# SwiGLU on one core: the first two tiles loaded, multiplied and stored row by row

## The chip, the cores and the metric

One core of one Trainium2 chip. The metric is the time of one execution on the device in microseconds (us), the median of several runs. The profile is of one execution; its span runs from the first to the last instruction and is 1 to 2 us shorter than the time. A packet is the piece of a transfer that one DMA engine moves in one go, here what lies together in one partition: 64 KiB in a whole load, 32 KiB in a whole store. Where the text says "packet records", the start and duration of every packet were read from the trace file; no view of the profile prints them.

## The reference

```python
"x": np.random.randn(8192, 8192).astype(np.float32)

def reference(x):
    a, b = np.split(x, 2, axis=-1)
    silu_b = b / (1 + np.exp(-b))
    return a * silu_b
```

Every row of 8192 floats (32 KiB) gives a row of 4096 floats (16 KiB): 268.4 MB are read and 134.2 MB written. ScalarE makes the SILU of the right half, VectorE multiplies it by the left.

## The kernel before

The input is seen as 4096 pairs of rows, the pairs cut into 32 tiles of 128. One tile holds two rows (64 KiB) in each of the 128 partitions, 8.39 MB in all. There are three tile buffers. Loads and the last three stores go out on SyncE's queue (SP), the other thirty stores on ScalarE's (ACT). The product is written over the tile itself, so a buffer is free for the next load only when its store has landed. The last tile is already loaded and stored by rows; the first tiles are not.

```python
R = 2
BUFS = 3
...
def load(i, rows=None):
    if i not in tiles:
        tiles[i] = pool.tile([P, R * M], x.dtype, name="xt")
    lo, hi = (0, R) if rows is None else rows
    nc.sync.dma_start(
        out=tiles[i][:, lo * M : hi * M], in_=xv[i * P : (i + 1) * P, lo * M : hi * M]
    )

def swiglu(i, k, c0=0, cw=half):
    xt = tiles[i]
    b = xt[:, k * M + half + c0 : k * M + half + c0 + cw]
    nc.scalar.activation(out=b, in_=b, func=_SILU)
    nc.vector.tensor_mul(
        out=xt[:, k * half + c0 : k * half + c0 + cw],
        in0=xt[:, k * M + c0 : k * M + c0 + cw],
        in1=b,
    )

def store(i, c0=0, cw=R * half):
    (nc.scalar if i < last - 1 else nc.sync).dma_start(
        out=ov[i * P : (i + 1) * P, c0 : c0 + cw], in_=tiles[i][:, c0 : c0 + cw]
    )

for i in range(BUFS):
    load(i)
for i in range(last):
    for k in range(R):
        swiglu(i, k)
    if i == last - 1:
        swiglu(last, 0)
    store(i)
    nxt = i + BUFS
    if nxt < last:
        load(nxt)
    elif nxt == last:
        load(last, (0, 1))
        load(last, (1, 2))
... # the last tile: store of row 0, row 1 in two halves, store of row 1
```

Of the kernel before, what the change touches and what calls it, by code (L numbers as in the profile page):

```python
# [1 line left out]

# [4 lines left out]

_SILU = mybir.ActivationFunctionType.Silu


@with_exitstack
def kernel(
    ctx: ExitStack,
    tc: tile.TileContext,
    x: bass.AP,
    out: bass.AP,
):




    nc = tc.nc
    N, M = x.shape
    half = M // 2
    P = nc.NUM_PARTITIONS
    R = 2
    BUFS = 3

    xv = x.tensor.reshape([N // R, R * M]).ap()  # L30
    ov = out.tensor.reshape([N // R, R * half]).ap()
    ntiles = N // (P * R)
    last = ntiles - 1

    pool = ctx.enter_context(tc.tile_pool(name="sbuf", bufs=BUFS))
    ctx.enter_context(tc.manual_schedule())
    tiles = {}
# [22 lines that stand above are left out]
        )  # L60

    for i in range(BUFS):
        load(i)
    for i in range(last):
        for k in range(R):
            swiglu(i, k)
        if i == last - 1:
            swiglu(last, 0)
        store(i)
        nxt = i + BUFS  # L70
        if nxt < last:
            load(nxt)
# [4 lines that stand above are left out]
    store(last, 0, half)  # L77
    for c0 in range(0, half, half // 2):
        swiglu(last, 1, c0, half // 2)
    store(last, half, half)  # L80


# [1 line left out]
_INS = ['x']  # L84
_OUTS = [((8192, 4096), 'float32')]


# [23 lines left out]
```

## Time and profile before

| | before |
|---|---|
| time, median (lowest to highest) | 936.18 us (936.04 to 936.34) |
| span of the profiled run | 934.8 us |
| both DMA queues, share of 16 engines | 99.8% |
| VectorE, ScalarE busy | 30%, 25% |
| HBM traffic over the span | 431 GB/s |

The engines that compute have little to do; the 16 DMA engines are busy all the time. In this list of DMA issues of the kernel before, the last number is the median time from issue to landing in us:

```profile
out_dram<-xt ACTq DMA_DIRECT2D x30, 4096.0 KB, 39.7
...
xt<-in_x_dram SPq DMA_DIRECT2D x31, 34.5
```

A whole load (8 MiB, its size isn't printed) takes 34.5 us and a store of 4 MiB takes 39.7, though alone, at 434 GB/s, they would take 19.3 and 9.7. They wait for each other in the queues.

### The profile page before, as it was taken

The page shows a single profiled execution, that of the slowest core. Times are in us where ns is not written, and L with a number is a line of the kernel's source. Part 1 is how long each engine was busy: PE and PEld are TensorE (multiplying, and loading weights), DVE is VectorE, ACT ScalarE, POOL GpSimd, SP SyncE. Part 2 cuts the span into 40 slices and gives each one's busy share as a digit, 9 for nine tenths or more (in the row PEclk, how much of TensorE's full clock was granted, in tenths as well). Part 3 has the DMA queues.
Part 4 walks back from the last instruction along what each step waited for, and adds up shares of the span by engine and source line. Part 5 has one row for each costly group of instructions (what it writes and reads, how often), then busy time and mean ns, then how long its engine had stood idle before and what let it go on. Part 6 is the DMA issues. An engine that isn't in the chain of part 4 may idle for free.

```text
span 934.8 us, 367 instructions
## 1 busy us (share of the span) xinstructions
DVE 283.3 (30%) x65; ACT 229.4 (25%) x66; POOL 0.2 (0%) x4
## 2 busy tenths in 40 slices
DVE  0333312333123331133321333213332133331242
ACT  0223320233302333113331133311333203332041
POOL 0000000000000000000000000000000000000000
DMA  9999999999999999999999999999999999999998
GB/s 404 400 445 430 430 439 433 428 435 443 428 430 439 429 442 432 435 426 453 419 430 452 411 452 423 428 447 425 433 433 453 414 443 429 426 447 428 425 437 376
DMA packets 9506, 402.67 MB, mean 431 GB/s; under 512 B 1056, under 2 KB 1056, under 8 KB 1056
## 3 DMA queue, kind: packets, MB, share of 16 engines
q1 hardware_dynamic: 5184, 276.83, 68.6%
q10 hardware_dynamic: 4320, 125.83, 31.2%
q14 instruction: 2, 0.02, 0.0%
HBM read 268.44 MB, written 134.22 MB: 431 GB/s over the span
## 4 chain that ended last, share of the span: by engine, by line
DMA 84%; DVE 10%; ACT 4%; DVEq 0%; issue 0%; SPq 0%; ACTq 0%
DMA out_dram<-xt 42%; DMA xt<-in_x_dram 42%; DVE xt L51 10%; ACT xt L50 4%; DVEq L106 0%; SPq L43 0%; ACTq L50 0%; DVEq L51 0%
## 5 line engine op out<-in xcount | busy, mean ns | idle before, releaser
L51 DVE TENSOR_TENSOR xt<-xt 128x4096 f32<-128x4096 f32 (+1 forms) x65 | 283.3, 4359 | 637.7 <-ACT xt L50 634.5
L50 ACT ACTIVATE xt<-xt 128x4096 f32<-128x4096 f32 (+1 forms) x65 | 228.1, 3556 | 688.1 <-DMA xt<-in_x_dram 688.1
L50 ACT ACT_TABLE_LOAD x1 | 1.3, 1283 | 0.7 <-PEq L95 0.7
L95 POOL MEMSET const-bfloat16-1.0<- 128x1 bf16 x1 | 0.1, 103 | 0.0
L95 POOL MEMSET const-uint8-127<- 128x1 uint8 x1 | 0.1, 102 | 0.0
L95 POOL MEMSET const-float32-0.0<- 128x1 f32 x1 | 0.1, 100 | 0.2 <-issue 0.2
L95 POOL MEMSET const-float32-1.0<- 128x1 f32 x1 | 0.1, 99 | 0.0
## 6 DMA issues: line engine op xcount, KB each, us to landing
out_dram<-xt ACTq DMA_DIRECT2D x30, 4096.0 KB, 39.7
xt<-in_x_dram SPq DMA_DIRECT2D x2, 4096.0 KB, 27.1
out_dram<-xt SPq DMA_DIRECT2D x1, 4096.0 KB, 23.6
out_dram<-xt SPq DMA_DIRECT2D x2, 2048.0 KB, 14.5
xt<-in_x_dram SPq DMA_DIRECT2D x31, 34.5
```

The lines of the kernel that those rows point to most:

```text
L50: nc.scalar.activation(out=b, in_=b, func=_SILU)
L51: nc.vector.tensor_mul(out=xt[:, k * half + c0 : k * half + c0 + cw], in0=xt[:, k * M + c0 : k * M + c0 + cw], in1=b,)
L95: nc = _bacc.Bacc("TRN2", target_bir_lowering=False, num_devices=1)
```

## The change

The intent: ScalarE gets its first data only after 22.6 us and the first store is issued at 35.2 us. With the first two tiles cut into rows, and each row's compute into halves, the pipeline fills sooner, as the kernel already empties sooner at the other end.

```diff
     BUFS = 3
+    BY_ROWS = 2
...
     for i in range(BUFS):
-        load(i)
+        if i < BY_ROWS:
+            for k in range(R):
+                load(i, (k, k + 1))
+        else:
+            load(i)
     for i in range(last):
         for k in range(R):
-            swiglu(i, k)
+
+            step = half // 2 if i < BY_ROWS else half
+            for c0 in range(0, half, step):
+                swiglu(i, k, c0, step)
+            if i < BY_ROWS:
+                store(i, k * half, half)
         if i == last - 1:
             swiglu(last, 0)
-        store(i)
+        if i >= BY_ROWS:
+            store(i)
```

## The prediction

> **What bounds the kernel now.** I read the busy shares and the DMA queues first, then a table of stretches (to find where the rate is lower), then the timeline of the head and of the tail, and last the groups by shape for the prices.
>
> ```profile
> DVE 283.3 (30%) x65; ACT 229.4 (25%) x66; POOL 0.2 (0%) x4
> ...
> q1 hardware_dynamic: 5184, 276.83, 68.6%
> q10 hardware_dynamic: 4320, 125.83, 31.2%
> ...
> HBM read 268.44 MB, written 134.22 MB: 431 GB/s over the span
> ```
>
> The two queues (q1 is SP's: the loads and the last three stores; q10 is ACT's: thirty stores) take 68.6 + 31.2 = 99.8% of the time of the 16 DMA engines. No engine that computes is above 30%. So the kernel is a copy at the DMA's pace, and all idle DMA time together is 0.2% of 934.8 us, about 1.9 us. The span is the sum of the packets' times plus a start and an end.
>
> Where is the pace lower? The columns are stretch, length, busy us of VectorE, ScalarE and GpSimd, clock, DMA share, GB/s; packets are booked where they start, so short stretches jitter.
>
> ```profile
> 0.00:20.90 20.90, 0.00 (x0) 1.28 (x1) 0.20 (x4) 1.00 0.96 401
> 20.90:38.00 17.10, 8.85 (x2) 7.12 (x2) 0.00 (x0) 1.00 1.00 429
> 38.00:48.00 10.00, 0.00 (x0) 1.56 (x1) 0.00 (x0) 1.00 0.98 367
> 48.00:900.00 852.00, 264.92 (x60) 212.11 (x60) 0.00 (x0) 1.00 1.00 434
> ```
>
> 434 GB/s holds for 91% of the span. The first 20.9 us run at 401, short by 20.9 x 33/434 = 1.6 us: the single packet records show the first data packet at 1.7 us and the first packets at some 3.2 us instead of 2.4. The stretch from 38 to 48 us is at 367, short by 10 x 67/434 = 1.5 us: there the packets of the first store begin (issued at 35.2, first packet at 39.5), and the load packets beside them take up to 4.1 us. Between the two, with loads alone in flight and no store, the rate is 429: reading alone is not slower than reading and writing. The head has about 3 us that could ever be won.
>
> The head, then the tail, in the timeline (start, duration, what, idle time before):
>
> ```profile
> 0.73 98.56 SPq L43 DMA_DIRECT2D xt<-in_x_dram  x5
> 22.61 7.12 ACT L50 ACTIVATE xt<-xt 128x4096 f32<-128x4096 f32 x2 [20.60 <-DMA xt<-in_x_dram]
> 26.25 8.96 DVE L51 TENSOR_TENSOR xt<-xt 128x4096 f32<-128x4096 f32 x2 [26.25 <-ACT xt L50]
> 35.24 0.37 ACTq L58 DMA_DIRECT2D out_dram<-xt  x1
> 46.44 7.12 ACT L50 ACTIVATE xt<-xt 128x4096 f32<-128x4096 f32 x2 [16.71 <-DMA xt<-in_x_dram]
> ...
> 75.42 7.12 ACT L50 ACTIVATE xt<-xt 128x4096 f32<-128x4096 f32 x2 [21.87 <-DMA xt<-in_x_dram]
> ...
> 900.62 20.71 SPq L58 DMA_DIRECT2D out_dram<-xt  x3
> 904.92 3.62 ACT L50 ACTIVATE xt<-xt 128x4096 f32<-128x4096 f32 x1 [9.80 <-DMA xt<-in_x_dram]
> ...
> 914.53 3.71 ACT L50 ACTIVATE xt<-xt 128x2048 f32<-128x2048 f32 x2 [6.00 <-DMA xt<-in_x_dram]
> 916.47 4.50 DVE L51 TENSOR_TENSOR xt<-xt 128x2048 f32<-128x2048 f32 x2 [3.48 <-ACT xt L50]
> ```
>
> ScalarE and VectorE idle 22.6 and 26.3 us at the start, and the first store is issued only at 35.2. That looks like a pipeline fill worth shortening, and is what the change is after. But three loads of 8.39 MB are queued from 0.7 us: 25.2 MB, 58 us of DMA work at 434 GB/s. The engines that matter never wait for the fill.
>
> The groups by shape give the prices:
>
> ```profile
> L51 DVE TENSOR_TENSOR xt<-xt 128x4096 f32<-128x4096 f32 x63 | 278.8, 4425 | 634.2 <-ACT xt L50 631.0
> L50 ACT ACTIVATE xt<-xt 128x4096 f32<-128x4096 f32 x63 | 224.4, 3608 | 682.1 <-DMA xt<-in_x_dram 682.1
> L51 DVE TENSOR_TENSOR xt<-xt 128x2048 f32<-128x2048 f32 x2 | 4.5, 2288 | 3.5 <-ACT xt L50 3.5
> L50 ACT ACTIVATE xt<-xt 128x2048 f32<-128x2048 f32 x2 | 3.7, 1901 | 6.0 <-DMA xt<-in_x_dram 6.0
> ```
>
> **What the Trainium skill says.** "DMA: Bandwidth & Descriptors", section "Bandwidth", under "Where 436 GB/s comes from", puts the ceiling of the 16 ports at 435.2 GB/s. The trace agrees: 434 over 852 us, so no better order of transfers can raise the pace. The same page, "Queues, rings and completion order", says that each DMA engine goes round its queues packet by packet. The trace agrees: beside stores of 32 KiB packets, tile 2's load of 64 KiB packets needs 75.42 - 46.44 = 29.0 us for 8.39 MB, 289 GB/s, two thirds of 434. "Anatomy of one DMA" gives about 2 us fixed per DMA (a fit for DMAs issued from GpSimd), most of it waiting for completion. With 99.8% busy it is not exposed here, because other transfers are queued behind it. "Rules for kernel authors" asks for at least 1 MiB per DMA for full bandwidth; the new transfers are 4 MiB and 2 MiB.
>
> **The change part by part.**
>
> 1. Loads of tiles 0 and 1: two DMAs of 8 MiB become four of 4 MiB, 256 packets of 64 KiB become 512 of 32 KiB. The packet records give a median of 2418 ns for 64 KiB, 1213 for 32 KiB and 611 for 16 KiB. So +256 x (2 x 1213 - 2418) = 2.0 us of packet time, over 16 engines +0.13 us.
> 2. Stores of those tiles: 256 packets of 32 KiB become 512 of 16 KiB: 256 x (2 x 611 - 1213) = 2.3 us, over 16 engines +0.14 us.
> 3. Four more DMAs, each with 16 closing packets of 9 ns: 4 x 9 ns = +0.04 us per engine. The issue itself (0.33 us each) is on sequencers that wait anyway.
> 4. Compute: eight half-row pairs for four row pairs. ScalarE 8 x 1.901 - 4 x 3.608 = +0.8 us, VectorE 8 x 2.288 - 4 x 4.425 = +0.6 us. Both idle for over 600 us in all and are off the path: 0.
> 5. What moves. A row is 8 packets per engine, 8 x 1.213 = 9.7 us, so row 0 is there 8 x 2.418 - 9.7 = 9.6 us before the whole tile was: about 13.0. One ScalarE half (1.9) and two VectorE halves (4.6) later, at about 19.5, the first store is issued instead of at 35.2. Row 1 comes at about 22.7, its store at about 29.3. Store packets of 16 KiB alternate with load packets of 32 KiB, 0.611 + 1.213 = 1.82 us a pair. With the first store packet at about 22.5 to 23.5, some 17 of the 32 packets per engine of tiles 0 and 1 are in. The two stores of tile 0 then need 8 pairs, 7 pairs, and one pair with a 64 KiB packet of tile 2 (3.03 us): 14.6 + 12.8 + 3.0 = 30.4 us. So the buffer of tile 0 is free, and the fourth load issued, at about 54 instead of 69.9. Then tile 1's 16 packets alternate with 64 KiB packets, one to four, 3.03 us each: 16 x 3.03 = 48 us, and the fifth load comes at about 102, where it is now (98.96). The gain in phase is given back to the small stores' small share of the rotation. Through all this one queue or the other has work, so none of it changes the sum.
> 6. The end. The last load, on SP's queue, has behind it on the same queue the store of tile 30 (4.19 MB) and of row 0 of tile 31 (2.10 MB): 6.29 MB, 14.5 us. Row 1 of tile 31 needs after its landing 914.53 to 920.97, some 6.5 us, before its store, which is ready well inside those 14.5. So the tail ends at the DMA's pace and hides any shift of phase from the head. 0.
>
> Sum: 0.13 + 0.14 + 0.04 = +0.3 us: 936.18 + 0.3 = 936.5 us.
>
> **Rivals.** (a) The fill is on the path: the first store comes 35.2 - 19.5 = 15.7 us earlier and the kernel ends so much earlier, 920.5 us (-1.7%). For it: 22.6 us of idle ScalarE and a chain of waits that starts with a 45 us load. Against: DMA share 0.96 and 1.00 in just these stretches; at most the 1.9 us idle and some 3 us of slow packets exist, and the start of the first load doesn't move. (b) Small transfers pay a fixed cost: 4 more DMAs by about 2 us (the skill's figure) is 944 us (+0.9%). Against: packet times are in proportion to size, and the queues are full. (c) The 367 GB/s stretch: if the beginning of stores costs less beside smaller packets, up to 1.5 us are won (about 935); if it comes back for each kind of packet, 1.5 are lost (about 938). I can't tell which from this trace, and it makes most of the range. (d) The one-to-four rotation holds the small stores back so long that the load queue runs dry: then stores have the engines to themselves, which is still work at full rate; 0. Even (a) and (b) whole stay within 2%.
>
> **Range and chances.** The three runs of before lie within 0.3 us. To the +0.3 I add -1.2 and +1.5 for (c) and the noise: 935.3 to 938.0. For over 2%, 18.7 us, something must happen for which the profile has no room: a gain would need ten times the idle DMA time there is; a loss would need a new stall of the queues. Within 2%: 0.985.
>
> **What would show it right or wrong.** In the changed profile: DMA queues together again at about 99.8%, with 256 more load packets and 256 more store packets (and 64 closing ones); first SILU at about 13, first store at about 19.5, fourth load at about 54, fifth near 100; from 150 us on 434 GB/s and the same 29 us per tile; the last VectorE half still some 13 us before the end. Wrong, if the queues' share falls by more than 0.5%, if a stretch after the head is below 430 GB/s, or if the end comes more than 2 us sooner: then reading alone was dearer than its 429 GB/s says.

## The result and the profile after

936.81 us median (936.56 to 937.58, 4 runs) against 936.26 us (936.04 to 936.64, 4 runs): ratio 1.0007, 95% interval 0.9989 to 1.0024. That is the same time. (Ratios are the mean time of one kernel's runs over that of the other's of the same rounds, so not quite the ratio of the medians quoted.)

From the page after: the busy engines and the DMA queues:

```profile
DVE 283.5 (30%) x69; ACT 230.0 (25%) x70; POOL 0.2 (0%) x4
...
q1 hardware_dynamic: 5472, 276.83, 68.6%
q10 hardware_dynamic: 4608, 125.83, 31.2%
```

There are 288 more packets on each queue, as worked out (256 of data and 32 closing ones), and the shares have not moved: 68.6 + 31.2 = 99.8% of a span that is again 934.8 us.

The timeline of the changed kernel (start, duration, what, idle time before; the second and third fence are SP's own timeline in two windows, the fourth is SP's in the kernel before, again in two windows):

```profile
12.79 3.71 ACT L51 ACTIVATE xt<-xt 128x2048 f32<-128x2048 f32 x2 [10.78 <-DMA xt<-in_x_dram]
14.73 4.49 DVE L52 TENSOR_TENSOR xt<-xt 128x2048 f32<-128x2048 f32 x2 [14.73 <-ACT xt L51]
19.26 0.38 ACTq L59 DMA_DIRECT2D out_dram<-xt  x1
...
52.23 3.71 ACT L51 ACTIVATE xt<-xt 128x2048 f32<-128x2048 f32 x2 [10.83 <-DMA xt<-in_x_dram]
...
76.41 7.12 ACT L51 ACTIVATE xt<-xt 128x4096 f32<-128x4096 f32 x2 [20.48 <-DMA xt<-in_x_dram]
...
902.47 18.30 SPq L59 DMA_DIRECT2D out_dram<-xt  x3
...
915.92 4.49 DVE L52 TENSOR_TENSOR xt<-xt 128x2048 f32<-128x2048 f32 x2 [3.53 <-ACT xt L51]
```

```profile
0.73 52.07 SPq L44 DMA_DIRECT2D xt<-in_x_dram  x6
```

```profile
100.79 0.33 SPq L44 DMA_DIRECT2D xt<-in_x_dram  x1
```

```profile
69.94 0.33 SPq L43 DMA_DIRECT2D xt<-in_x_dram  x1
...
98.96 0.33 SPq L43 DMA_DIRECT2D xt<-in_x_dram  x1
```

The change does what it was made for. The first SILU is 9.8 us earlier (12.79 for 22.61), the first store 16.0 us (19.26 for 35.24). The sixth SP issue, which is the load of tile 3, ends at 52.80, so it began at about 52.5: 17 us earlier than the 69.94 of before. And then it is gone. Tile 2 is ready for ScalarE at 76.41 instead of 75.42, and the load of tile 4 is issued at 100.79 instead of 98.96. At the other end the last multiplication is over at 920.41 (before 920.97) and the issue of the last store ends at 920.77, with some 13 us of queued stores still to move (by the packet records the last one ends at 933.0). Nothing of the head start comes through.

The stretches of the head, after, same columns as in the prediction:

```profile
0.00:20.90 20.90, 4.49 (x2) 4.99 (x3) 0.20 (x4) 1.00 0.97 401
20.90:38.00 17.10, 4.49 (x2) 4.02 (x3) 0.00 (x0) 1.00 0.95 399
38.00:48.00 10.00, 4.49 (x2) 3.39 (x2) 0.00 (x0) 1.00 1.02 439
48.00:900.00 852.00, 258.69 (x60) 210.25 (x60) 0.00 (x0) 1.00 1.00 434
```

The stretch of lower pace (367 GB/s from 38 to 48 us before) has moved with the first store into the stretch from 20.9 to 38 (399), and 38 to 48 is now at 439. From 48 us on both kernels run at 434 GB/s. In the single packet records, the time of packets over their size's median is 2.2 us per engine before and 1.8 after.

The DMA issues, after:

```profile
out_dram<-xt ACTq DMA_DIRECT2D x28, 4096.0 KB, 32.5
...
xt<-in_x_dram SPq DMA_DIRECT2D x29, 41.7
```

A trap for a reader of profiles: a store now lands 7.2 us sooner and a load 7.2 us later, in the whole steady state, not in the head alone. But 39.7 + 34.5 = 74.2 and 32.5 + 41.7 = 74.2. With the 12.6 us of compute that is 86.8 us for one round of a buffer, three tiles of 29 us each. The change left the three buffers standing a little differently to each other, so waiting moved from one queue to the other. How long a transfer waits in a full queue says nothing of the time.

### The profile page after: what moved, and what is told of

Read it like the earlier page. It is cut to its first block, busy times and chain, and to the rows that moved or that the text cites. A ratio compares the mean times of both kernels' runs of the same rounds, so it can differ in the third digit from the quotient of the medians.

```text
span 934.8 us, 387 instructions
## 1 busy us (share of the span) xinstructions
DVE 283.5 (30%) x69; ACT 230.0 (25%) x70; POOL 0.2 (0%) x4
## 3 DMA queue, kind: packets, MB, share of 16 engines
q1 hardware_dynamic: 5472, 276.83, 68.6%
q10 hardware_dynamic: 4608, 125.83, 31.2%
## 4 chain that ended last, share of the span: by engine, by line
DMA 83%; DVE 10%; ACT 4%; another core or an unknown queue 1%; issue 0%; DVEq 0%; SPq 0%; ACTq 0%
DMA xt<-in_x_dram 47%; DMA out_dram<-xt 36%; DVE xt L52 10%; ACT xt L51 4%; DVEq L117 0%; SPq L44 0%; ACTq L59 0%; ACTq L51 0%; DVEq L52 0%
## 5 line engine op out<-in xcount | busy, mean ns | idle before, releaser
L52 DVE TENSOR_TENSOR xt<-xt 128x4096 f32<-128x4096 f32 (+1 forms) x69 | 283.5, 4115 | 636.9 <-ACT xt L51 633.9
## 6 DMA issues: line engine op xcount, KB each, us to landing
out_dram<-xt ACTq DMA_DIRECT2D x28, 4096.0 KB, 32.5
out_dram<-xt SPq DMA_DIRECT2D x2, 2048.0 KB, 14.5
xt<-in_x_dram SPq DMA_DIRECT2D x29, 41.7
```

What stands on the lines that cost most here:

```text
L52: nc.vector.tensor_mul(out=xt[:, k * half + c0 : k * half + c0 + cw], in0=xt[:, k * M + c0 : k * M + c0 + cw], in1=b,)
```

## The experiments

In the expectations, theory 1 is the prediction's account, and rivals A and B are its rivals (a) and (b).

**1. The loads alone by rows (e1_loads_by_rows).** Compute and stores stay whole.

```diff
 # against the kernel before
     for i in range(BUFS):
-        load(i)
+        if i < BY_ROWS:
+            for k in range(R):
+                load(i, (k, k + 1))
+        else:
+            load(i)
```

> Only the loads of tiles 0 and 1 are split into rows; compute and stores stay whole. Theory 1 (the DMA engines are never idle, the sum of packet times sets the end): +0.13 us for the packets and +0.02 for two more DMAs, so 936.4 us, ratio 1.000; the first SILU at about 13, the first store (it waits for row 1) at about 22.7 + 3.6 + 2 x 4.4 = 35, as before. Rival A (the fill is on the path and its gain was eaten by an equal cost of small stores): the cost of the small stores is gone, but so is the early store; 936. Rival B (2 us for every further DMA): 940.

Measured: 936.3 us (936.23 to 937.43, 5 runs) against 936.25, ratio 1.0003, interval 0.9991 to 1.0016. As theory 1 has it, though a gain and a cost that cancel were not told apart by this run; 2 us per DMA (940) is out. One part of the expectation was a slip: the first store was issued at 30.7, not 35. With row 0 landed early its multiplication is over before row 1 comes, so only row 1's 3.6 + 4.4 us stand between its landing (22.6) and the store. Thus a third start of the stores, 30.7 beside 35.2 and 19.3, and again the same time.

**2. Every tile by rows (e2_all_by_rows).** The dose taken 15.5 times.

```diff
 # against the changed kernel
-    BY_ROWS = 2
+    BY_ROWS = 31
...
         if nxt < last:
-            load(nxt)
+            for k in range(R):
+                load(nxt, (k, k + 1))
```

> Tiles 0 to 30 are all loaded, multiplied and stored by rows: the dose of the change taken 15.5 times. Theory 1: 31 tiles x 8 packets per engine x (8 ns for loads + 9 ns for stores) = 4.2 us, and 62 more DMAs x 9 ns = 0.6 us: 936.2 + 4.8 = 941.0 us, ratio 1.005; both DMA queues together still at 99.8% of the span. Rival A: the fill gives the same once, the small packets' cost 15.5 times over; if that cost were as large as the fill's supposed 15.7 us per two tiles, over 1100. Rival B (about 2 us fixed per DMA exposed): 62 x 2 = 124 us more, 1060.

Measured: 938.69 us (938.59 to 939.16, 5 runs) against 936.25, ratio 1.0027, interval 1.0015 to 1.004. Its DMA queues:

```profile
q1 hardware_dynamic: 9792, 276.83, 68.6%
q10 hardware_dynamic: 8640, 125.83, 31.4%
```

So small packets do cost, but +2.4 us (1.4 to 3.7 by the interval), half of the 4.8 expected, and nowhere near the rivals' 1060 or 1100. Spread over 15.5 pairs of tiles it is 0.16 us for what the change did, or 0.2 us if the 0.8 us that slow packets took less here (below) are counted as a gain of their own. Where the other half went is in the packet records: the packets' durations add up to 4.0 us more per engine than before, but the two shares now add up to 100.0% of a span that is only 2 us longer. Recorded durations of successive packets overlap a little, and the more packets there are, the more: what is in flight beyond 16 packets for 16 engines adds up to 1.7 us per engine before and to 3.6 us here. (The remaining 0.8 of the 4.8 are slow packets: 1.4 us of them here, 2.2 before.) The sum of recorded durations overstated what the small packets cost.

**3 and 4. The first store put off by 15 and by 40 us.** The change's intent backwards: extra SILUs on a scratch tile hold ScalarE between the two rows of tile 0.

```diff
 # against the kernel before; HOLD = 8 and HOLD = 21
+    scratch = ctx.enter_context(tc.tile_pool(name="scratch", bufs=1)).tile([P, half // 2], x.dtype, name="scratch")
+    nc.gpsimd.memset(scratch[:, :], 0.0)
...
             swiglu(i, k)
+            if i == 0 and k == 0:
+                for _ in range(HOLD):
+                    nc.scalar.activation(out=scratch[:, :], in_=scratch[:, :], func=_SILU)
```

> Eight extra half-row SILUs on a scratch tile, 1.9 us each, between the two row SILUs of tile 0 put off the first store by 15.2 us, from 35.2 to about 50.4: the change's head start, backwards. Theory 1: the three loads of the head keep the DMA engines busy to about 60 us and the store begins before that, so nothing is lost: 936.2 us, ratio 1.000, queues 99.8%. Rival A (the start of the stores is on the path): 951.

Measured: 936.03 us (935.66 to 936.34, 5 runs) against 936.25, ratio 0.9997, interval 0.9984 to 1.0011. Its first store, from the timeline:

```profile
49.69 0.37 ACTq L61 DMA_DIRECT2D out_dram<-xt  x1
```

14.5 us later than in the kernel before, at no cost whatever. This is the run that decides for theory 1 against "a gain eaten by a cost": there is no cost of small transfers in it that could hide anything, and the start of the stores counts for nothing in either direction.

> The same with 21 extra SILUs: first store at about 75.1. Theory 1: the 25.2 MB of loads are through at about 60.4 (1.74 + 25.17 MB / 433.9 GB/s + 0.6 for the slow first packets), then the DMA engines stand idle to about 77.1 (2 us after the issue), 16.7 us; store 0 alone takes 9.7 us and the second store and the fourth load begin only at about 90, 3.2 us more idle. Together +20 us: 956, ratio 1.021; the queues' share falls to about 97.7%. Rival A: +40, so 976. If the time is still 936, the stores are not needed at all for the pace.

Measured: 953.84 us (953.67 to 954.01, 4 runs), ratio 1.0189, interval 1.0175 to 1.0202: +17.6 us. The queues and the stretches around the hole in this kernel:

```profile
q1 hardware_dynamic: 5184, 276.83, 67.4%
q10 hardware_dynamic: 4320, 125.83, 30.6%
```

```profile
60.00:76.00 16.00, 4.43 (x1) 10.99 (x6) 0.00 (x0) 1.00 0.08 33
76.00:86.00 10.00, 6.95 (x2) 6.42 (x2) 0.00 (x0) 1.00 0.86 367
86.00:90.00 4.00, 1.90 (x1) 1.68 (x1) 0.00 (x0) 1.00 0.74 262
90.00:100.00 10.00, 7.93 (x2) 5.44 (x2) 0.00 (x0) 1.00 1.04 419
```

Here the head does count. The three loads are through at about 60 us, the DMA engines stand still (share 0.08) until the first store, and the page's queues fall to 98.0%. By the packet records the two holes are 60.6 to 75.8 and 85.6 to 87.3, together 16.9 us, and the rest of the 17.6 is of the size of the slow packets after them. Expected were 16.7 + 3.2 for the holes: the first store's packets followed 0.9 us after its issue, not 2 (in the kernel before, with loads in flight, 4.3 us: 35.24 to 39.5). So of the 39.6 us of delay some 24 should be free, as a first store issued by about 59.7 would still meet the end of the loads at 60.6; the other 15 cost 17.6, with the second hole and the slow packets. This is worked out from the trace; no run lies between 49.7 and 74.9. The head of the original kernel has this much slack to spare, and a head start added to slack is worth nothing.

**5, 6 and 7. Two buffers instead of three.** If only idle DMA time counts, row by row work should pay in a kernel that has some. One buffer fewer makes one: the kernel before with `BUFS = 2` (e5), the changed kernel with `BUFS = 2` (e6), and the all-by-rows kernel of experiment 2 with `BUFS = 2` (e7).

```diff
-    BUFS = 3
+    BUFS = 2
```

> The kernel before with 2 tile buffers instead of 3, to have a kernel whose DMA engines do run dry. Theory 1 (only idle DMA time counts): after each store has landed there is one buffer in compute (12.6 us from landing to the issue of its store, some 2 us more to its first packet) and one load just issued; by a hand walk the engines have some 3 to 4 us without work per tile, 32 tiles: about 936 + 32 x 3.5 = 1050 us (1000 to 1080), queues at about 89%. If the third buffer is not what hides the compute, 936.

Measured: 1049.95 us (1049.36 to 1050.23, 4 runs), ratio 1.1212. Its queues and its steady state:

```profile
q1 hardware_dynamic: 5184, 276.83, 66.4%
q10 hardware_dynamic: 4320, 125.83, 27.8%
```

```profile
150.00:900.00 750.00, 203.57 (x46) 162.96 (x46) 0.00 (x0) 1.00 0.94 384
```

The time is the expected one, its make-up is not, so that the number was met is luck. The queues are at 94.2% and not 89%: 94.2% of the span of 1047.6 us is 987 us of packet time, where the kernel before needed 99.8% of 934.8, 933 us, for the very same packets. Idle engines are only about half of the loss; the other half is slower packets. The packet records say where these are. In 30 holes of mostly 1.7 to 2 us the engines are idle, about 60 us in all between the first packet and the last. The 30 times at which the load queue starts again after it had been empty, the packets of the next 3 us take 20.1 us over their size's median (summed and divided by 16 engines), 0.7 us per start. The 30 times at which the store queue starts, it is 34.2 us, 1.1 us per start, counted from 5 us before its first packet to 3 us after; it is load packets that are slow there, while store packets keep their median. This is the pattern of the slow stretch from 38 to 48 us of the kernel before, 1.5 us in its packet records, now once per tile. In the kernel before, each queue is started once, and after that neither goes longer than 3.1 us without a packet. That the slow packets come with the starts is shown; why is open.

> The change itself (first two tiles by rows) on the kernel with 2 buffers. Theory 1: the head of the two-buffer kernel has at most about 2 us of idle engines before the steady state (41 us of loads cover the first store at 35), so the change again is worth 0 to 4 us against e5_two_buffers. Rival A (an earlier first store moves the whole pipeline up wherever the pipeline is not saturated): up to 15 us less than e5_two_buffers.

Measured: 1045.19 us (1044.89 to 1049.07, 4 runs) against e5's 1049.95, both against the same runs of the kernel before (ratios 1.1175 and 1.1212). That is 4.8 us less by the medians and 3.5 us by the ratios, which take in the one slower run of 1049.07; the intervals (1.1152 to 1.1199 and 1.1196 to 1.1229) still touch, so a gain is likely but not shown beyond doubt. It is at the upper end of what theory 1 allowed, far from the 15 of rival A. The packet records show one hole fewer (29 against 30): e5's first, from 52.4 to 54.9 us, is not there. The spans differ by 4.3 us; the records have 1.3 us less idle and 3.5 us less packet time, so most of it is not the idle time on which the expectation counted.

> 2 buffers, all of tiles 0 to 30 by rows. Theory 1: splitting by rows pays where the engines run dry for want of a store: row 0's store is in the queue while row 1 is still loading and computing, and the last row needs 6.5 us instead of 12.6 to its store. The idle time per tile falls from 3 to 4 us to about 0 to 1: 945 to 975 us, clearly under e5_two_buffers, and not under 936. Rival B (each DMA has an exposed fixed cost): above e5_two_buffers.

Measured: 941.06 us (940.3 to 941.63, 4 runs), ratio 1.005, interval 1.0035 to 1.0065. Its queues:

```profile
q1 hardware_dynamic: 9792, 276.83, 68.6%
q10 hardware_dynamic: 8640, 125.83, 31.3%
```

Under the range of 945 to 975: the holes are not fewer but gone, save one of 0.7 us near 896. Row by row work takes 109 us off the two-buffer kernel, and brings it to within 2.4 us of the three-buffer one with all tiles by rows (938.69, from other rounds), with 64 KiB per partition of memory to spare. The same edit is worth 10% where the DMA engines run dry, and costs 0.3% where they don't (experiment 2). Which of its parts, loads, compute or stores by rows, closes the holes was not tested. No version beats the kernel before: at 99.8% there is no room.

## Why the prediction was right, point by point

- **Bound.** The step "all idle DMA time together is about 1.9 us" carried the forecast, and the trace after shows the same 99.8%. The 1.9 us themselves are too low: the first data packet starts at 1.7 us and the last ends 1.2 us before the end of the span, 2.9 us together, and overlapping durations fill the share up again. That is still far too little for a gain of 15.7. Experiments 3 and 4 show it by moving the first store the other way: 14.5 us later cost nothing, 39.6 us later cost 17.6.
- **Steps 1 to 3, the small packets: +0.31 us.** The sign fits the dose of experiment 2, the size was one and a half times to twice too big: 2.4 us over 15.5 pairs of tiles, so 0.16 to 0.2 us for the change. The term that was mis-sized is the duration of a packet taken as its cost; successive packets overlap. The +0.55 between the medians is inside the noise (the interval of the ratio is about 1.7 us either way), and no run separates it from 0.2 or from 0.
- **Step 4, compute.** +0.8 and +0.6 us were forecast for ScalarE and VectorE; the page has +0.6 (229.4 to 230.0) and +0.2 (283.3 to 283.5), as two halves back to back overlap: a pair on VectorE takes 4.49 us and not 2 x 2.29. Off the path either way.
- **Step 5, what moves.** First SILU 13.0 forecast, 12.79 measured; first store 19.5 and 19.26; the load of tile 3 at 54 and 52.5; the load of tile 4 at 102 and 100.8. The rotation packet by packet fits the return: beside stores of 16 KiB packets the load of tile 2 (64 KiB packets) ran from 52.2 to 76.4, 8.39 MB in 24.2 us, 347 GB/s, four fifths of 434, so small stores got a fifth.
- **Step 6, the end.** The last multiplication is over 13 us before the last store's bytes are through, as forecast.
- **The rivals.** (a), the fill on the path: refuted by experiments 3 and 4. (b), a fixed cost per DMA: refuted by experiment 2, where 62 more DMAs cost 2.4 us in all. (c), the slow stretch: it belongs to the first store and moves with it, and was 0.7 us instead of 1.5 in the packet records (over the whole run, slow packets took 1.8 us instead of 2.2); so less than half a microsecond was won there. Experiment 5 shows it again at the restarts of a queue. Why it is slow is open. (d), the load queue runs dry: it did, when tile 3 had landed (ScalarE started on it at 100.63) and tile 4's load was only then issued (100.79): no load packet runs from 99.6 to 104.9 us. As forecast it cost next to nothing, since stores had the engines to themselves (DMA share 1.04 from 99.6 to 104.9); the slow packets at the restart are 0.3 us.
- **"From 150 us on the same 29 us per tile".** Right, though the phase of the buffers did change (the 7.2 us from stores to loads); that it would, the prediction had not said.

## What to carry to other kernels

Before shortening a pipeline's fill, look at what the bounding resource does in it: here the queued loads kept the DMA engines busy to 60 us, so the first store could come anywhere from 19 to 50 us for the same time. Work in smaller pieces pays where the bounding resource runs dry while it waits for a piece (two buffers: 1050 to 941 us), and there it can stand in for a buffer. A transfer's time from issue to landing is no measure of speed when the queues are full. The share of the queues says more, but it counts slow packets as busy: with two buffers it fell from 99.8% to 94.2% while the time grew by 12%; the GB/s (431 to 384) show both.

## What the Trainium skill lacked or had wrong

- "DMA: Bandwidth & Descriptors", section "Anatomy of one DMA": the roughly 2 us fixed per DMA (stated for DMAs issued from GpSimd) is right to be left out of a sum where the queues are full, and the section's formula doesn't say so. 62 more DMAs, and the smaller packets that came with them, cost 2.4 us in all, about 0.04 us each (at most 0.06 by the interval).
- The same page, nowhere: what it costs when a queue starts again after being empty. With two buffers, packets after a restart of the load queue took 0.7 us in all over their median (30 restarts), and around a start of the store queue 1.1 us (30 starts), together about half of what the missing buffer cost.
- The same page, "Queues, rings and completion order": round robin by packets is stated, but not what follows for the shares when packets differ. 32 KiB stores beside 64 KiB loads left the load 289 GB/s of 434, 16 KiB stores left it 347. In these two mixes the shares went as the packet sizes.
- "HBM Reference", section "Specifications (TRN2)", speaks of about 425 GB/s for a core streaming alone; a mix of reads and writes held 434 GB/s over 852 us here, within 0.3% of the 435.2 ceiling of the DMA page.
- No page says of a trace that the durations of DMA packets overlap slightly, so that their sum overstates the time. With 16 and 32 KiB packets the sum rose by 4.0 us per engine and the span by 2.0.
